# Two retention steps beside each group of scans, and the output projection's weights on the other side of SBUF

## The chip, the core and the metric

The kernel runs on one NeuronCore of one Trainium2 chip as a single launch. The metric is the device time of one execution in microseconds (us). Every execution has five engines with a queue each: TensorE (PE; its weight loads are listed as PEld), VectorE (DVE), ScalarE (ACT), GpSimd (POOL) and SyncE (SP), which issues most of the transfers between HBM and the on-chip memory SBUF.

## The reference

Two transformer blocks over 1024 tokens of width 1024. The part that matters here is the middle of the first block: a token mixer with two halves, whose results are joined, projected and routed to experts.

```python
def token_mix(h, hc, w_in, ..., w_out, need_ctx):
    u, uc = h @ w_in, hc @ w_in
    ret_lat, ret_ctx = retention_group(u[..., :RET_COLS], uc[..., :RET_COLS], need_ctx)
    rw = depthwise_conv(u[..., RET_COLS:], conv_w)
    rwc = depthwise_conv(uc[..., RET_COLS:], conv_w)
    rwkv_lat, rwkv_ctx = rwkv_group(rw, rwc, w0, w2, a0, a2, g2, k_k, k_a, r_k, lnx_w, lnx_b, need_ctx)
    lat = jnp.concatenate([ret_lat, rwkv_lat], axis=-1).astype(h.dtype) @ w_out
...
def first_block(...):
        x = x + gt1 * rms_norm(mix, g_post_mix)
        h2 = rms_norm(x, g_pre_ffn) * (1.0 + sc2) + sh2
        x = x + gt2 * rms_norm(ec_moe(h2, w_router[i], w_gate[i], w_up[i], w_down[i]), g_post_ffn)
```

`retention_group` is linear attention with a fixed decay per head in both directions over chunks of 128 tokens. `rwkv_group` is a recurrent scan, `S = S * w + (S a) b + v k`, in both directions; its result is normalised, gated (`g_f`, `g_b`) and added. `mix` is the product with `w_out`; `ec_moe` picks tokens by a router and runs 16 experts.

## The kernel before, in words

The kernel is written as Python generators whose code order is the program order; a scheduler then sets the order in each engine's queue, and each queue runs strictly in that order. Tiles come from pools. A pool lies on the left or on the right side of SBUF; a pool opened later on the same side takes the memory that an earlier one gave back, and its first write waits until the last reader of that memory is done.

The scan (`phase_chain`) is cut into 20 groups: 4 head pairs times one context group and 4 latent groups of 4 chunks of 64 tokens (names such as `UT_331` are group 3, pair 3, direction 1). A group has a preparation for each direction (scores `psc`, transposes `pb` and `pa`, the products `pm`, `px`, `pw`, `pg`, ending in `GQ`) and then four steps of the state: two products into `pc` (L826, L830) and the decay on VectorE, `S` (L835). ScalarE copies the outputs to `yst`, and SP stores them to `Yd` (L848, two transfers for each latent group; context groups store nothing). These pools lie on the left.

The retention (`phase_retention`) is a generator of 20 steps, 10 for each half of the heads: one rotates the keys (`kT`, L909), one builds the chunk states (`KV`, L917 to L930), and eight work on 128 tokens each (the score product `rs`, L957; the store to `LatD`, L986). On the token steps with odd index it also runs one of eight parts of `phase_mod2` (L204 to L216), which computes rows that scale the mix. Its pools lie on the right. The first 6 groups run beside the end of the input projection. The last 14 run beside the retention, by the loop in `first`: 1 step after an even group, 2 after an odd one, so 20 steps end with the last group.

`phase_out` follows. `gates(blk)` prepares 256 tokens: it loads `LatD`, the gate inputs `SGd`, `Yd` and `BV`, and makes the transposed left operand `lTh` and `lTl` (high and low halves) in two stages `q`, each with a square, a sum, a power on GpSimd, a product (`gyn`, L1057), a transpose (`yT`, L1063) and the gating (`z`). The output weights `w_out` come in 8 pieces (`woraw`); each is split into a high part by ScalarE (`wohi`) and a low part (`wolo`) by GpSimd for the first 4 and by VectorE for the other 4. The product is three matmuls for each piece into `mo`; ScalarE copies the result to `mix` (L1152), and norms, router, top-k and experts follow. Two tiles of 128 tokens make one block, and each tile has two halves of 512 columns. In this version the pools of the gates (`gnC`, `gnT`, `ouL`) lie on the right, where the retention was, and those of the weights, of the output tiles and of the rows (`ouW`, `ouT`, `ouG`) on the left, where the scan was.

Of the kernel before, what the change touches and what calls it, by code (L numbers as in the profile page):

```python
# [878 lines left out]
def phase_retention(E, A, tabs, others):  # L879
# [15 lines left out]
    for hh in range(2):  # L895
# [40 lines left out]
        for t in range(8):  # L936
            q = tp.tile([P, 1, 4, C], F32, tag="q", name=f"q{hh}_{t}s")
            nc.gpsimd.dma_start(q.rearrange("p o h d -> p (o h d)"), E.RD["q"][t * P:(t + 1) * P, cols])
            do_rope(q, t, 1, f"q{hh}_{t}")
            pk = bank(f"qTp{hh}_{t}")  # L940
            for j in range(2):
                nc.tensor.transpose(pk[:, j * P:(j + 1) * P], q[:, 0, 2 * j:2 * j + 2].rearrange("p h d -> p (h d)"), E.ident)
            qT, kv = qTs[t % 2], kvs[t % 2]
            qd = tp.tile([P, 2, 2, P], F32, tag="qd", name=f"qd{hh}_{t}")
            pkv = pk[:, :256].rearrange("p (j t) -> p j t", j=2)
            sp = (9 if t == 0 else t - 1, 8 if t == 7 else t + 1)
            for h in range(2):
                hs = slice(64 * h, 64 * h + 64)
                nc.scalar.copy(qT[hs, :, h], pkv[hs])
                for d in range(2):  # L950
                    nc.scalar.copy(kv[hs, :, d, h], KV[hs, :, sp[d], d])
            for d in range(2):
                nc.vector.tensor_mul(qd[:, d], pkv, qdec[:, 2 * hh:2 * hh + 2, d])
            psc = bank(f"rs{hh}_{t}")
            sv = psc.rearrange("p (j h t) -> p j h t", j=2, h=2)
            for j in range(2):
                nc.tensor.matmul(sv[:, j].rearrange("p h t -> p (h t)"), kT[:, t, j, :],  # L957
                                 qT[:, j].rearrange("p h t -> p (h t)"), start=True, stop=True)
            pm = tp.tile([P, 2, 2, 2, P], F32, tag="pm", bufs=1, name=f"pm{hh}_{t}")
            for j in range(2):  # L960
                for h in range(2):
                    nc.vector.tensor_mul(pm[:, j, h], sv[:, j, h].unsqueeze(1).to_broadcast([P, 2, P]),
                                         dmask[:, 4 * hh + 2 * j + h])
            yb = bank(f"y_{hh}_{t}")
            yv = yb.rearrange("p (h d v) -> p h d v", h=4, d=2)
            for j in range(2):
                for d in range(2):
                    nc.tensor.matmul(yv[:, 2 * j:2 * j + 2, d], qd[:, d, j], kv[:, j, d], start=True, stop=False)
                    for h in range(2):
                        nc.tensor.matmul(yv[:, 2 * j + h, d], pm[:, j, h, d], vt[:, t, 2 * j + h, :], start=False, stop=h == 1)  # L970
            nc.scalar.copy(Y[:, t], yv)
            sq = tp.tile([P, 8, C], F32, tag="ysq", bufs=1, name=f"ysq{hh}_{t}")
            yv = Y[:, t].rearrange("p h d v -> p (h d) v")
            nc.scalar.activation(sq, yv, AF.Square)
            ss = tp.tile([P, 8], F32, tag="yss", name=f"yss{hh}_{t}")
            nc.vector.tensor_reduce(ss, sq, axis=AX.X, op=OP.add)
            r = rstd_col(E, tp, ss, 8, 1.0 / C, 1e-6, f"yr{hh}_{t}")
            nc.vector.tensor_mul(yv, yv, r.unsqueeze(2).to_broadcast([P, 8, C]))
            g = tp.tile([P, 2, 4, C], F32, tag="gs", name=f"gs{hh}_{t}")
            for d in range(2):  # L980
                nc.gpsimd.dma_start(g[:, d].rearrange("p h v -> p (h v)"), E.RD["fb"[d]][t * P:(t + 1) * P, cols])
            nc.scalar.activation(g, g, AF.Silu)
            for d in range(2):
                nc.gpsimd.tensor_mul(g[:, d], g[:, d], Y[:, t, :, d, :])
            nc.vector.tensor_add(g[:, 0], g[:, 0], g[:, 1])
            nc.gpsimd.dma_start(E.LatD[t * P:(t + 1) * P, cols], g[:, 0].rearrange("p h d -> p (h d)"))  # L986
            if t % 2:
                others.pop(0)()
            yield


def phase_out(E, A):
# [3 lines left out]
    nc, tc = E.nc, E.tc  # L996
    with ExitStack() as st:
        pt = st.enter_context(tc.tile_pool(name="ouP", bufs=2, space=PSUM))
        cst = st.enter_context(tc.tile_pool(name="gnC", bufs=1, side="right"))
        tp = st.enter_context(tc.tile_pool(name="gnT", bufs=2, side="right"))  # L1000
        pg = st.enter_context(tc.tile_pool(name="gnP", bufs=2, space=PSUM))
        lp = st.enter_context(tc.tile_pool(name="ouL", bufs=2, side="right"))
        wp = st.enter_context(tc.tile_pool(name="ouW", bufs=1))
        py = st.enter_context(tc.tile_pool(name="gnY", bufs=1, space=PSUM))
        to = st.enter_context(tc.tile_pool(name="ouT", bufs=2))
        po = st.enter_context(tc.tile_pool(name="ouO", bufs=2, space=PSUM))
        rp = st.enter_context(tc.tile_pool(name="ouG", bufs=1))

        g2 = cst.tile([P, 2, 2, 2, 2, C], F32, name="g2")
        for d in range(2):  # L1010
# [74 lines left out]
                    split_hl(E, zv[:, 0], lTh[:, 4 + h + 2 * q], lTl[:, 4 + h + 2 * q])  # L1085
            return lTh, lTl

        lT = [gates(0)]
        wo = A.w_out[0]
        rw = wo[512:1024].rearrange("(p h v) f -> p h v f", p=NPAIR, h=2)  # L1090
        wts = []
        for k in range(KD):
            raw = wp.tile([P, D], F32, tag="raw", bufs=3, name=f"woraw{k}")
            hi = wp.tile([P, D], F32R, name=f"wohi{k}")
            lo = wp.tile([P, D], F32R, name=f"wolo{k}")
            if k < 4:
                nc.sync.dma_start(raw, wo[k * P:(k + 1) * P])
            else:
                h, q = k % 2, (k - 4) // 2 * 2
                for a in range(2):  # L1100
                    nc.sync.dma_start(raw[64 * a:64 * a + 64], rw[q + a, h])
            nc.scalar.copy(hi, raw)
            (nc.gpsimd if k < 4 else nc.vector).tensor_sub(lo, raw, hi)
            wts.append((hi, lo))
        g1 = bc_row(E, rp, 0, "g1row")
        s2r = bc_row(E, rp, 1, "s2row")
        sh2 = bc_row(E, rp, 2, "sh2row")
# [1362 lines left out]
def first(E, A):  # L2470
    nc, tc, ctx = E.nc, E.tc, E.ctx
    dt = lambda n: E.dram.tile([T, D], F32, name=n)
    E.x1d, E.h2d, E.accd = dt("x1d"), dt("h2d"), dt("accd")
    E.Td = [E.dram.tile([64, C, C], F32, name=f"Td{g}") for g in range(5)]
    E.gv = E.const.tile([P, 16], F32, name="gv")
    E.idx = E.const.tile([P, 16], I32, name="idx")
    with tc.tile_pool(name="rwk", bufs=1) as E.rwk:


        with ExitStack() as st:  # L2480
            ent = st.enter_context
            E.hpool = ent(tc.tile_pool(name="hp", bufs=1, side="right"))
            wide = ExitStack()
            in_project(E, A, (ent(tc.tile_pool(name="inW", bufs=1, side="right")), ent(tc.tile_pool(name="inE", bufs=3, side="right")),
                              wide.enter_context(tc.tile_pool(name="inP", bufs=4, space=PSUM, side="right"))))
            E.pss = ExitStack()
            E.ps_small = E.pss.enter_context(tc.tile_pool(name="pssm", bufs=1, space=PSUM))
            start(E, A)
            last = phase_in(E, A)
            wide.close()  # L2490
            E.in_pools = E.in_pools[:2] + (ent(tc.tile_pool(name="inP2", bufs=2, space=PSUM, side="right")),)
            cs = ExitStack()
            run = phase_chain(E, A, cs)
            for i, f in enumerate(last):
                if i % 4 == 0:
                    next(run)
                f()
        with ExitStack() as E.rst:
            E.rps = E.rst.enter_context(tc.tile_pool(name="reP", bufs=2, space=PSUM, side="right"))
            tabs = ret_setup(E)  # L2500
            ret = phase_retention(E, A, tabs, phase_mod2(E, A))
            for i, _ in enumerate(run):
                for _ in range(1 + i % 2):
                    next(ret, None)
            for _ in ret:
                pass
            cs.close()
    E.const = ctx.enter_context(tc.tile_pool(name="const2", bufs=1))
    E.mks = ctx.enter_context(ExitStack())
    E.mkp = E.mks.enter_context(tc.tile_pool(name="mkv", bufs=1))  # L2510
    with tc.tile_pool(name="ap", bufs=1) as ap_:
        E.affT = ap_.tile([64, T // 2], F32, name="affT")
        phase_out(E, A)
        with tc.tile_pool(name="tkT", bufs=1) as tk, tc.tile_pool(name="tkP", bufs=1, space=PSUM) as tkp:
            phase_topk(E, tk, tkp)
            setup2(E, A, tk)
    phase_moe1(E, A)
# [91 lines left out]
```

## Time and profile before

| | us |
|---|---|
| median of 3 runs (4094.79 to 4105.12) | 4097.06 |
| profiled execution, its own time | 4104.47 |
| its span, first to last instruction | 4102.7 |
| TensorE busy | 3776.7 (92%) |
| VectorE busy | 2718.3 (66%) |
| ScalarE busy | 2135.5 (52%) |
| GpSimd busy | 826.6 (20%) |

The table gives the average over stages that differ. The change touches the stretch from about 797 us (the first group beside the retention) to about 1426 us (the end of the output projection). A row of a stretch gives its length, then for TensorE, its weight loads, VectorE, ScalarE and GpSimd in this order the busy time and, in brackets, the count of instructions; then the granted TensorE clock as a share of full speed, the busy share of the transfer engines and GB/s. In a timeline a row begins with the start and the length; the end in square brackets is idle time of that engine before it, and what ended it.

### The profile page before, as it was taken

How to read it: one execution, taken by the hardware profiler on the slowest of the kernel's cores; microseconds unless marked ns; L12 is line 12 of the kernel's file. 1: busy time of each engine (PE TensorE's matmuls, PEld its weight loads, DVE VectorE, ACT ScalarE, POOL GpSimd, SP SyncE). 2: the span in 40 equal slices, each digit the busy share in tenths (PEclk: the TensorE clock that was granted, in tenths of full speed). 3: DMA queues.
4: the chain of work that ended last, by engine and by line, in shares of the span. 5: the costliest groups of instructions: out<-in, count | busy, mean ns of one | idle time of the engine just before them, and what ended most of it. 6: DMA issues, size and time to landing. Idle time of an engine off the chain costs nothing. (4 is left out here: it accounts for less than half of the span.)

```text
span 4102.7 us, 61718 instructions
## 1 busy us (share of the span) xinstructions
PE 3776.7 (92%) x23138; PEld 3126.6 (76%) x23138; DVE 2718.3 (66%) x4777; ACT 2135.5 (52%) x3389; POOL 826.6 (20%) x1054
## 2 busy tenths in 40 slices
PE   7989889898887889999969998999998999999998
PEld 5777788777766658777747788898886777788876
DVE  4576774377766578888865413667644356899987
ACT  4443312232324357777668513667643243788886
POOL 2333420244434120010010001222200022221110
PEclk9999999998998899999989999999999999999999
DMA  7556554455445489999741122111125326899998
GB/s 249 155 173 182 156 136 105 136 138 145 110 117 171 163 341 382 385 379 378 254 150 49 53 62 69 34 50 37 38 66 182 134 72 223 316 382 387 382 382 305
DMA packets 503960, 782.78 MB, mean 191 GB/s; under 512 B 199697, under 2 KB 334810, under 8 KB 502506
## 3 DMA queue, kind: packets, MB, share of 16 engines
q1 hardware_dynamic: 412298, 610.50, 42.5%
q0 software_dynamic: 40816, 138.37, 11.5%
q10 hardware_dynamic: 50544, 29.92, 2.4%
q8 instruction: 184, 3.01, 0.3%
q14 instruction: 118, 0.97, 0.1%
HBM read 646.28 MB, written 132.43 MB: 190 GB/s over the span
## 5 line engine op out<-in xcount | busy, mean ns | idle before, releaser
L2327 DVE TENSOR_TENSOR m2l<-m2r,m2h 128x1024 fp32r<-128x1024 f32 x380 | 449.6, 1223 | 52.5 <-ACT m2h L2326 48.5
L1260 DVE TENSOR_TENSOR m1l<-m1r,m1h 128x2048 fp32r<-128x2048 f32 x189 | 427.2, 2289 | 70.6 <-ACT m1h L1259 68.9
L2326 ACT CAST m2h<-m2r 128x1024 fp32r<-128x1024 f32 x384 | 394.7, 1051 | 84.2 <-PE m2g L109 35.6
L1259 ACT CAST m1h<-m1r 128x2048 fp32r<-128x2048 f32 x192 | 362.6, 1918 | 109.1 <-PE gu L109 81.4
L108 PE MATMUL m2g<-m2l,m2thx 128*128 128x512 f32 x512 | 202.5, 395 | 1.3 <-DVE m2l L2327 0.8
L107 PE MATMUL m2g<-m2h,m2thx 128*128 128x512 f32 x512 | 202.9, 405 | 0.3 <-ACT m2h L2326 0.3
L109 PE MATMUL m2g<-m2h,m2tlx 128*128 128x512 f32 x512 | 201.5, 393 | 0.0
L108 PE MATMUL gu<-m1l,xh 128*128 128x512 f32 x512 | 200.1, 396 | 0.2 <-DVE m1l L1260 0.2
L109 PE MATMUL gu<-m1h,xl 128*128 128x512 f32 x512 | 199.0, 394 | 0.0
L107 PE MATMUL gu<-m1h,xh 128*128 128x512 f32 x512 | 181.8, 397 | 10.1 <-ACT xh L60 6.0
L107 PE MATMUL apqk<-atW_hi,hT2h 128*128 128x256 f32 x512 | 145.2, 284 | 0.0
L108 PE MATMUL apqk<-atW_lo,hT2h 128*128 128x256 f32 x512 | 145.0, 283 | 0.0
L109 PE MATMUL apqk<-atW_hi,hT2l 128*128 128x256 f32 x512 | 144.8, 283 | 0.0
L107 PE MATMUL u_ps<-hTh,inW_hi 128*128 128x512 f32 (+1 forms) x336 | 128.3, 382 | 6.7 <-ACT inW_hi L91 6.7
L2379 POOL DMA_INDIRECT out_dram<-m2y,did x32 | 68.9, 2153 | 297.7 <-ACT m2y L2378 297.7
L108 PE MATMUL u_ps<-hTl,inW_hi 128*128 128x512 f32 (+1 forms) x336 | 125.9, 375 | 0.1
L109 PE MATMUL u_ps<-hTh,inW_lo 128*128 128x512 f32 (+1 forms) x336 | 124.9, 373 | 0.0
L107 PEld LDWEIGHTS gu<-m1h,xh 128*128 128x128 f32 x512 | 94.8, 188 | 34.3 <-ACT xh L60 8.1
L108 PEld LDWEIGHTS gu<-m1l,xh 128*128 128x128 f32 x512 | 96.4, 188 | 27.5 <-DVE m1l L1260 7.6
L108 PEld LDWEIGHTS m2g<-m2l,m2thx 128*128 128x128 f32 x512 | 96.8, 189 | 24.6 <-DVE m2l L2327 5.9
L1697 DVE TENSOR_SCALAR_CACHE_REDUCE pr<-sc 128x512 f32<-128x512 f32 (+2 forms) x192 | 103.7, 551 | 17.1 <-PE sc L1693 14.4
L1281 POOL DMA_INDIRECT accd<-y,idx x16 | 28.7, 1794 | 418.9 <-ACT y L1280 383.5
(1216 smaller groups left out, 11655.1 us busy)
## 6 DMA issues: line engine op xcount, KB each, us to landing
m2r<-in_w_gate_up_dram SPq DMA_DIRECT2D x128, 1024.0 KB
m1r<-in_w_gate_dram SPq DMA_DIRECT2D x64, 1024.0 KB
m1r<-in_w_up_dram SPq DMA_DIRECT2D x64, 1024.0 KB
m1r<-in_w_down_dram SPq DMA_DIRECT2D x64, 1024.0 KB
m2r<-in_w_down_dram SPq DMA_DIRECT2D x64, 1024.0 KB
inW_raw<-in_w_in_dram SPq DMA_DIRECT2D x72, 256.0 KB
m2w<-in_w_mod_dram POOLq DMA_DIRECT2D x32, 512.0 KB, 4.5
luW_raw<-in_w_in_dram SPq DMA_DIRECT2D x24, 512.0 KB
```

What stands on the lines that cost most here:

```text
L107: nc.tensor.matmul(ps, lh, rh, start=start, stop=False)
L108: nc.tensor.matmul(ps, lh, rl, start=False, stop=False)
L109: nc.tensor.matmul(ps, ll, rh, start=False, stop=stop)
L1259: nc.scalar.copy(hi, raw)
L1260: (nc.gpsimd if i < 3 else nc.vector).tensor_sub(lo, raw, hi)
L1281: nc.gpsimd.indirect_dma_start(out=E.accd, out_offset=bass.IndirectOffsetOnAxis(ap=E.idx[:, e:e + 1], axis=0), in_=y, in_offset=None, comp ...
L1697: nc.vector.tensor_scalar(pr[:, m, n0:n1], ps[m][:, :n], -1.0, None, op0=OP.mult, op1=OP.min, accum_out=s[:, 4 * i + m:4 * i + m + 1])
L2326: nc.scalar.copy(hi, raw[:, j])
L2327: (nc.gpsimd if i in (0, 2) else nc.vector).tensor_sub(lo, raw[:, j], hi)
L2379: nc.gpsimd.indirect_dma_start(out=E.x4d, out_offset=bass.IndirectOffsetOnAxis(ap=col, axis=0), in_=y, in_offset=None, compute_op=OP.add)
```

## The change

Three edits. After each of the last 14 groups the loop takes 2 steps of the retention, so its 20 steps stand beside 10 groups and the last 4 groups have none. The parts of `phase_mod2` run on even token steps instead of odd ones. In `phase_out` the two sets of pools change sides, and the code that loads and splits the weights stands ahead of `gates(0)`.

```diff
@@ phase_retention
-            if t % 2:
+            if t % 2 == 0:
                 others.pop(0)()
@@ phase_out
-        cst = st.enter_context(tc.tile_pool(name="gnC", bufs=1, side="right"))
-        tp = st.enter_context(tc.tile_pool(name="gnT", bufs=2, side="right"))
+        cst = st.enter_context(tc.tile_pool(name="gnC", bufs=1))
+        tp = st.enter_context(tc.tile_pool(name="gnT", bufs=2))
...
-        lp = st.enter_context(tc.tile_pool(name="ouL", bufs=2, side="right"))
-        wp = st.enter_context(tc.tile_pool(name="ouW", bufs=1))
+        lp = st.enter_context(tc.tile_pool(name="ouL", bufs=2))
+        wp = st.enter_context(tc.tile_pool(name="ouW", bufs=1, side="right"))
...
-        to = st.enter_context(tc.tile_pool(name="ouT", bufs=2))
+        to = st.enter_context(tc.tile_pool(name="ouT", bufs=2, side="right"))
...
-        rp = st.enter_context(tc.tile_pool(name="ouG", bufs=1))
+        rp = st.enter_context(tc.tile_pool(name="ouG", bufs=1, side="right"))
...
-        lT = [gates(0)]
         wo = A.w_out[0]
...
             wts.append((hi, lo))
+        lT = [gates(0)]
@@ first
-            for i, _ in enumerate(run):
-                for _ in range(1 + i % 2):
+            for _ in run:
+                for _ in range(2):
                     next(ret, None)
```

SP's queue at the end of the scan, before. `yst33` and `yst43` are the outputs of the last two groups; `g2`, `lt`, `gsg`, `gy` and `bv` are loads of the first block of gates.

```order
L848 DMA Yd_5525<-yst33_12562 128x256 x2
L1014 DMA g2_13041<-in_rwkv_g2_dram 128x2x64 x8
L1034 DMA lt0_13065<-LatD_8535 128x512
L1042 DMA gsg0_13083<-SGd0_792 128x256
L1047 DMA gy00_13086<-Yd_5525 128x2x256 x2
L848 DMA Yd_5525<-yst43_12853 128x256 x2
L1072 DMA bv000_13113<-BV0_783 64x256
L1047 DMA gy01_13142<-Yd_5525 128x2x256 x2
L1097 DMA woraw0_13198<-in_w_out_dram 128x1024
```

The same place now (the last weight piece is in two halves, of which one stands ahead of the gates' loads and one behind).

```order
L1096 DMA woraw0_13063<-in_w_out_dram 128x1024
L1096 DMA woraw2_13075<-in_w_out_dram 128x1024
L848 DMA Yd_5525<-yst33_12703 128x256 x2
L1096 DMA woraw3_13081<-in_w_out_dram 128x1024
L1100 DMA woraw6_13101<-in_w_out_dram 64x1024 x2
L1014 DMA g2_13041<-in_rwkv_g2_dram 128x2x64
L848 DMA Yd_5525<-yst43_12936 128x256 x2
L1014 DMA g2_13041<-in_rwkv_g2_dram 128x2x64 x7
L1100 DMA woraw7_13108<-in_w_out_dram 64x1024
L1034 DMA lt0_13117<-LatD_8535 128x512
L1042 DMA gsg0_13135<-SGd0_792 128x256
L1047 DMA gy00_13138<-Yd_5525 128x2x256 x2
```

The weights moved from behind the last store of the scan to ahead of it, and the gates' loads, all but one piece of `g2`, from ahead of it to behind it.

VectorE's queue over the four state steps of the last group, before. `S430` to `S433` are the steps; `Y1`, `gs1_7` are the last token step of the retention, `m2b31` the last part of `phase_mod2`.

```order
L835 TENSOR_TENSOR S430_12861<-pc430_12854,PT4_5552 128x128 x2
L978 TENSOR_TENSOR Y1_11256<-Y1_11256,yr1_7_rstd_12951 128x512
L211 TENSOR_TENSOR m2b31_12979<-m2b31_12979,m2ps31_12981 1x512
L835 TENSOR_TENSOR S431_12873<-pc431_12866,PT4_5552 128x128 x2
L985 TENSOR_TENSOR gs1_7_12954<-gs1_7_12954 128x256
L1025 COPY lncols_13061<-lnps_13059 128x8
L835 TENSOR_TENSOR S432_12885<-pc432_12878,PT4_5552 128x128 x2
L215 SCALAR_TENSOR_TENSOR m2b31_12979<-m2b31_12979,m2a31_12962 1x512
L835 TENSOR_TENSOR S433_12897<-pc433_12890,PT4_5552 128x128 x2
```

The same place now.

```order
L835 TENSOR_TENSOR S430_12944<-pc430_12937,PT4_5552 128x128 x2
L1102 TENSOR_TENSOR wolo4_13089<-woraw4_13087,wohi4_13088 128x1024
L835 TENSOR_TENSOR S431_12956<-pc431_12949,PT4_5552 128x128 x2
L835 TENSOR_TENSOR S432_12968<-pc432_12961,PT4_5552 128x128 x2
L1102 TENSOR_TENSOR wolo5_13096<-woraw5_13094,wohi5_13095 128x1024
L835 TENSOR_TENSOR S433_12980<-pc433_12973,PT4_5552 128x128 x2
```

Two splits of the weights stand between the steps where parts of the retention and of `phase_mod2` stood.

## Rows read from the trace of the kernel before

**Rows 1.** Stretches: length, PE, PEld, DVE, ACT, POOL, clock, transfers.
```profile
640.00:735.00 95.00, 94.93 (x1043) 82.88 (x1043) 43.26 (x128) 24.25 (x68) 3.67 (x6) 1.00 0.39 101
797.00:1222.00 425.00, 379.55 (x3811) 311.19 (x3811) 319.50 (x828) 138.77 (x366) 174.64 (x222) 0.92 0.50 129
1222.00:1281.00 59.00, 36.42 (x128) 25.85 (x126) 34.58 (x46) 20.40 (x31) 24.54 (x14) 0.74 0.63 184
1281.00:1426.00 145.00, 127.31 (x632) 105.90 (x633) 84.52 (x161) 59.26 (x117) 34.06 (x32) 0.88 0.44 151
```
**Rows 2.** SP's timeline, stores of latent groups: start, length, operation.
```profile
667.63 0.82 SPq L848 DMA_DIRECT2D Yd<-yst  x2
...
704.15 0.82 SPq L848 DMA_DIRECT2D Yd<-yst  x2
...
827.22 1.10 SPq L848 DMA_DIRECT2D Yd<-yst  x2
849.41 1.62 SPq L848 DMA_DIRECT2D Yd<-yst  x2
...
911.45 0.80 SPq L848 DMA_DIRECT2D Yd<-yst  x2
...
1004.09 1.25 SPq L848 DMA_DIRECT2D Yd<-yst  x2
1040.99 0.81 SPq L848 DMA_DIRECT2D Yd<-yst  x2
1075.48 0.80 SPq L848 DMA_DIRECT2D Yd<-yst  x2
...
1222.57 1.59 SPq L848 DMA_DIRECT2D Yd<-yst  x2
```
**Rows 3.** Busy time by engine in two pairs of groups (columns as in the first group).
```profile
847.00:909.00 62.00, 56.64 (x583) 47.68 (x581) 48.46 (x135) 24.23 (x68) 25.23 (x33) 0.97 0.46 118
1004.00:1075.00 71.00, 61.40 (x622) 49.96 (x622) 55.21 (x142) 22.83 (x61) 31.05 (x36) 0.90 0.52 134
```
**Rows 4.** TensorE's timeline, first and last retention step of each pair.
```profile
855.20 1.13 PE L957 MATMUL rs<-rqT,kT 128*128 128x256 f32 x4
...
899.47 1.13 PE L957 MATMUL rs<-rqT,kT 128*128 128x256 f32 x4
...
1018.49 1.11 PE L909 MATMUL kTp<-ident,kt 128*128 128x128 f32 x4 [0.31 <-DVE kt L893]
...
1071.12 1.13 PE L957 MATMUL rs<-rqT,kT 128*128 128x256 f32 x4
```
**Rows 5.** SP's timeline, loads of the first block of gates.
```profile
1207.78 4.67 SPq L1014 DMA_DIRECT2D g<-in_rwkv_g_dram  x8
...
1219.51 0.96 SPq L1047 DMA_DIRECT2D gy<-Yd  x2
```
**Rows 6.** What TensorE waited for, 1222 to 1300 us: total, times, longest.
```profile
PE yT L1063 <- DVE gyn L1057: 13.1, 4, 6.3
PE mo L108 <- POOL wolo L1103: 5.6, 2, 4.3
PE mo L107 <- ACT wohi L1102: 4.8, 3, 2.6
```
**Rows 7.** ScalarE's timeline, second halves of the first two output tiles.
```profile
1267.10 0.59 ACT L1152 COPY mix<-mo 128x512 f32<-128x512 f32 x1 [0.27 <-PE mo L109]
...
1290.22 0.59 ACT L1152 COPY mix<-mo 128x512 f32<-128x512 f32 x1 [3.94 <-PE mo L109]
```
**Rows 8.** Timelines of VectorE and GpSimd, first block of gates and weight splits.
```profile
1231.09 1.29 DVE L1057 TENSOR_TENSOR gyn<-gy,gr_rstd 128x512 f32<-128x512 f32 x2 [2.19 <-POOL gr_rstd L118]
...
1244.46 5.59 DVE L1057 TENSOR_TENSOR gyn<-gy,gr_rstd 128x512 f32<-128x512 f32 x2 [2.79 <-POOL gr_rstd L118]
...
1263.71 1.22 DVE L1103 TENSOR_TENSOR wolo<-woraw,wohi 128x1024 fp32r<-128x1024 f32 x1 [3.58 <-ACT wohi L1102]
...
1244.40 7.86 POOL L1103 TENSOR_TENSOR wolo<-woraw,wohi 128x1024 fp32r<-128x1024 f32 x3
```

## Prediction

> **What bounds the kernel now.** I read the busy times by stretch first, then the spacing of SP's stores, the timelines of TensorE and VectorE, and TensorE's waits. The change touches two stages. In the first, 797 to 1222 us, scans run beside the retention; TensorE is busy 379.55 of 425 us, VectorE 319.50, at a granted clock of 0.92 [rows 1]. So TensorE is nearly the bound, and a better order can win at most the tenth that it idles. Earlier, from 640 to 735, scans ran beside the input projection with TensorE busy 94.93 of 95 [rows 1]; the stores at 667.63 and 704.15 enclose two groups, 36.52 us or 18.26 a group [rows 2]. That is my price of a group without retention, though matmuls of the projection are in it, so a group by itself may be shorter.
>
> The second stage is the output projection. Its first 59 us are thin: TensorE busy 36.42 at a clock of 0.74, then 127.31 of 145 [rows 1]. There TensorE waits 13.1 us for `gyn`, which the transposes `yT` need, and for the split weights 5.6 (GpSimd) and 4.8 (ScalarE) [rows 6]. The change removes the last two and makes the loads behind the first later.
>
> **Two steps beside a group.** No step is added or taken away; the same 20 stand otherwise. From the store at 827.22 to the last at 1222.57 are 395.35 us and 13 groups with 19 steps [rows 2]; 13 groups at 18.26 are 237.38, so a step beside a group costs (395.35 - 237.38)/19 = 8.31. If that holds for every step, the change moves the scan's end by nothing: what the last four groups save, the first ten pay.
>
> The new pattern, two steps a group, stands by chance in the old order as well: between the stores at 849.41 and 911.45 are two groups and four token steps (the score product at 855.20 opens the first, that at 899.47 the last), at a clock of 0.97 [rows 2 to 4]. 62.04 us less 36.52 leave 25.52, or 6.38 a step. Between 1004.09 and 1075.48 are also four, the rotation and the chunk states among them, at 0.90 [rows 2 to 4]: 71.39 less 36.52 are 34.87, or 8.72. The first of those groups alone, with those two steps, took 36.90 (to 1040.99) [rows 2]: 18.64 over 18.26, or 9.32 a step.
>
> Four steps of the 20 are of the rotating kind and 16 token steps; one falls before 827.22, so 15 token steps remain. At 8.72 and 6.38 they make 4 x 8.72 + 15 x 6.38 = 130.6, against 157.97 now: the scan would end 27.4 us earlier. All 19 at 8.72 make 165.7, 7.7 later; at 9.32, 177.1, 19.1 later. At the stage's clock the 62.04 would be 62.04 x 0.97/0.92 = 65.4, so 7.22 a token step and 143.2 in all, 14.7 earlier. I take half way between this and nothing, **-7 us**: TensorE's busy share in the dense pair, 56.64 of 62 or 91% [rows 3], is hardly above the stage's 89%, and idle time given to the last four groups is lost again.
>
> What hides nothing any more is the cover of those four groups: TensorE's waits in a state step (two products, the decay on VectorE, the next products) have had retention matmuls in them, and now have none.
>
> **The splits inside the scan.** `wolo4` and `wolo5` stand between the last four `S`, at 1.22 us each [rows 8], 2.44 in all. They take the place of five small operations, which the order shows, so I count 0. But what `wolo` costs beside GpSimd is not constant: the `gyn` pair took 1.29 us alone and 5.59 while GpSimd ran three of its `wolo` (7.86 from 1244.40) [rows 8], 4.33 times as long. GpSimd's four splits now run beside the end of the scan. Were both VectorE splits stretched so, they would take 10.6, 8.1 more. The page "GPSIMD Engine Reference" of the Trainium skill, section "8. Key points", says that the two engines share their access to SBUF and that VectorE instructions with two SBUF inputs suffer; `gyn` has two, and its two durations agree; the decays `S` read PSUM for one input and would be spared. ScalarE's six casts stand between the copies of the scan's outputs; ScalarE is busy 138.77 of 425 [rows 1], so I let them hide; if each held up a copy, and the copy the next product, by a `wolo`'s 1.22, it would be 7.3. Both bounds together are 0 to 15; I take **+2**, near the low end because the time between the `S` is mostly waiting.
>
> **The output projection.** Let E be the last `Yd` store, now 1222.57. The second halves of the first two tiles are copied at 1267.10 and 1290.22 [rows 7], E + 44.5 and E + 67.7. The weights no longer wait: they are asked for before E, in memory that the retention has left. The gates' loads, however, now follow the store. Before, `gy00` was issued at 1219.51, E - 3.1 [rows 5]. Now ahead of it stand the store (1.59) [rows 2], seven eighths of the `g2` loads (4.67 x 7/8 = 4.1) [rows 5], and half a weight piece, `lt` and `gsg`, at about a store's 0.8 each (estimated): E + 8.1, so 11.2 later. The first `gyn` pair ended at 1231.09 + 1.29, E + 9.8, and the second at 1244.46 + 5.59, E + 27.5 [rows 8]. The first goes to E + 21.0. The second followed by 17.7, of which 4.3 were the stretch beside GpSimd's `wolo`, gone now: E + 34.4.
>
> From there to the first tile's copy were 17.0, with most of the 10.4 of weight waits in them. Taking three quarters of these out gives 9.2 and the first tile at E + 43.6, 0.9 earlier. For the second tile: TensorE's 36.42 us at 0.74 are 27.0 at full speed, about 13.5 for each of the two tiles, so E + 57.1, 10.6 earlier. After that TensorE is busy 88% and catches only what it lacked, and the gates of the next block, issued late as well, can hold it. If nothing of the weight waits comes out, the first tile is 6.9 late; if all, 1.7 early, and the second tile's 10.6 may carry through whole. Bounds -11 to +7; I take **-5**.
>
> **Other edits.** The eight parts of `phase_mod2` run a step earlier each with the same instructions, hidden by VectorE's idle quarter: 0; if that cover is lacking in the dense groups it is in the step price above. After 1426 the order is the same, and later stages shift whole.
>
> Sum: -7 + 2 - 5 = -10 from the profiled execution's 4104.47, so 4094.5. The median is 7.4 below that execution; the same below gives **4087**.
>
> **Rivals.** First, the dense pattern is cheap (0.18). Steps cost 6.38 and the rotating ones 8.72, the scan ends 27.4 earlier, and with the rest (-3) the time is 4097 - 30 = 4067. For it: the pair at 62.04. Against: its clock of 0.97 was better than the stage's, and 15 such steps in a row have not been seen. A group by itself under 18.26 would lead there too, since four of them are left alone.
>
> Second, nothing is gained (0.20). Price 8.31 holds, so the dense groups pay what the thin ones save, and `gyn`, 11.2 later, takes the place of the weights as the wait before the first tile. Then 0 to +7: 4097 to 4104, 4100 as its value. For it: TensorE's waits were longer on `gyn` (13.1) than on the weights (10.4) [rows 6]. The change does what it says, but its prize is then hidden.
>
> Third, slower by crowding (0.10). The state steps queue on VectorE behind the operations of two retention steps, and each costs 9.32 as in the group up to 1040.99. The scan ends 19.1 later, and with -3 the time is 4113. It decides from the step price at which 19 steps outweigh the rest by the measurable amount: 8.31 + 15.3/19 = 9.1. For it: VectorE is busy 48.46 and 55.21 in the pairs, 78% [rows 3], with chained waits. Against: three of four groups seen were cheaper.
>
> Fourth, slower by a thin end (0.10). The last four groups, without filler, run at a lower granted clock. The stretch after 1222, where TensorE worked in bursts between waits, had 0.74, between the two levels of 1.2 and 2.4 GHz [rows 1]. At 0.74 a group costs 18.26/0.74 = 24.7, four of them 25.7 more; with the forecast's -10 that is 4113. It decides from a clock of 0.76: there 4 x 18.26 x (1/0.76 - 1) = 23 outweighs the forecast's gain and the measurable difference. The page "TensorE: Matmul & The Clock Gate", section "HAM oscillation — how this bites in real kernels", of the Trainium skill says that bursts between waits start throttled again and again; the 0.74 agrees with it, and by that rule this rival would be the likeliest. Against: in a group the waits are short ones of one engine for another, and with the scan the clock was 1.00 from 640 to 735 [rows 1], though with filler.
>
> **How the numbers follow.** The forecast has 0.42; its own range is 4078 to 4097, by -17 to +2 in the sum's terms. What a measurement tells from no change is about 0.3%, 12.3 us: 4084.8 to 4109.4. Of the forecast 0.19 lies below that and 0.23 inside, the first rival is faster, the second is the same, and the two slower ones count fully as slower: faster 0.37, same 0.43, slower 0.20. The range 4062 to 4113 leaves out the far half of the first rival's cheap end and of the two slow ones.
>
> **What would show it.** The stores in the first ten groups: spacing near 33 us is the forecast's (18.26 + 2 x 7.2 to 7.8), 31 the first rival, 35 the second, 37 the third. The last four: 18 to 19 us each at a clock above 0.9; 24 the fourth rival. The last store should stand some 5 us earlier. TensorE's waits on `wolo` and `wohi` should be gone, those on `gyn` longer, and the first two copies at E + 44 and E + 57. The forecast is wrong if the last store moves by over 15 either way, if the second copy is no closer to E than now, or if a stage after 1426 changes its own length.

## The result and the profile after

The changed kernel takes 4129.96 us (median of 5 runs, 4126.55 to 4131.69) against 4097.06 before; the ratio is 1.0072, 95% interval [1.0054, 1.0090]. It is slower; the forecast of 4087 and its range, which ended at 4113, were wrong.

The profiled executions, 4131.61 against 4104.47, are 27.1 us apart. By stage: the last `Yd` store comes 41.7 us later; from it to the last copy of the output projection are 176.0 us where there were 181.6, so 36.1 are left there; between 3076 and 3480 us, where both kernels have the same code, the distance falls from 36 to 27. That execution of the kernel before was 7.4 above its median, so I give this last difference no cause.

SP's stores of the scan in the changed kernel (start, length), which answer to [rows 2]:

```profile
829.12 0.81 SPq L848 DMA_DIRECT2D Yd<-yst  x2
859.37 0.80 SPq L848 DMA_DIRECT2D Yd<-yst  x2
896.61 0.80 SPq L848 DMA_DIRECT2D Yd<-yst  x2
928.93 0.95 SPq L848 DMA_DIRECT2D Yd<-yst  x2
1014.66 1.00 SPq L848 DMA_DIRECT2D Yd<-yst  x2
...
1130.24 0.82 SPq L848 DMA_DIRECT2D Yd<-yst  x2
1208.76 0.80 SPq L848 DMA_DIRECT2D Yd<-yst  x2
1228.52 0.80 SPq L848 DMA_DIRECT2D Yd<-yst  x2
1247.15 0.80 SPq L848 DMA_DIRECT2D Yd<-yst  x2
1264.28 0.93 SPq L848 DMA_DIRECT2D Yd<-yst  x2
```

Up to 1130.24 are 8 groups with 16 steps: (301.12 - 8 x 18.26)/16 = 9.69 a step, above the 8.31 of before. The next 78.5 us hold two groups and the end of the retention; then three groups stand 17 to 20 apart. Stretches of the same kernel, the columns as in [rows 1]:

```profile
829.10:1264.30 435.20, 363.43 (x3512) 297.63 (x3512) 297.33 (x774) 133.25 (x346) 164.41 (x203) 0.87 0.46 121
...
859.40:1130.20 270.80, 222.09 (x2037) 183.69 (x2036) 189.62 (x482) 82.71 (x218) 121.48 (x157) 0.85 0.50 129
1130.20:1190.00 59.80, 47.40 (x425) 35.49 (x425) 39.56 (x101) 13.02 (x31) 19.38 (x28) 0.77 0.29 81
1190.00:1264.30 74.30, 67.40 (x785) 56.97 (x785) 41.73 (x121) 23.89 (x62) 9.99 (x5) 1.00 0.44 122
1264.30:1323.00 58.70, 39.29 (x163) 31.11 (x164) 29.81 (x57) 17.91 (x30) 18.67 (x13) 0.83 0.55 166
1323.00:1465.00 142.00, 123.83 (x614) 101.01 (x613) 81.89 (x154) 57.05 (x114) 28.25 (x29) 0.89 0.42 144
```

and the stage of the scans in the kernel before, between the same two stores:

```profile
827.20:1222.60 395.40, 354.10 (x3530) 290.05 (x3531) 295.74 (x773) 127.80 (x343) 157.67 (x201) 0.91 0.49 127
```

TensorE idles 71.8 us of the stage (435.2 - 363.4) where it idled 41.3. Busy time times granted clock, an estimate of its work at full speed, is 322 before and 316 after: about the same work, done with more waits and at a lower clock. The clock is 0.85 where two steps stand beside a group (859 to 1130 us) and 1.00 behind them.

TensorE's waits in this stage (for whom: total, times, longest), after and then before:

```profile
PE pc L826 <- DVE S L835: 13.7, 16, 3.1
PE m2ps L210 <- DVE m2a L204: 12.6, 3, 6.0
PE pm L761 <- DVE UT L738: 6.9, 1, 6.9
...
PE pm L761 <- DVE UV L793: 6.1, 5, 1.7
```

```profile
PE pc L826 <- DVE S L835: 9.3, 9, 2.3
PE m2ps L210 <- DVE m2a L204: 4.0, 2, 2.8
...
PE pm L761 <- DVE UV L793: 2.3, 2, 2.1
```

Summed over all such rows, TensorE waits 54.5 us for VectorE after and 26.2 before. The longest shows how. VectorE's timeline at the place:

```profile
1163.78 0.75 DVE L204 SCALAR_TENSOR_TENSOR m2a<-m2w,cs,m2a 128x512 f32<-128x512 f32 x1
...
1166.12 0.69 DVE L978 TENSOR_TENSOR Y<-Y,yr_rstd 128x512 f32<-128x512 f32 x1
1166.73 0.75 DVE L204 SCALAR_TENSOR_TENSOR m2a<-m2w,cs,m2a 128x512 f32<-128x512 f32 x1
1168.77 0.43 DVE L985 TENSOR_TENSOR gs<-gs 128x256 f32<-128x256 f32 x1 [1.29 <-POOL gs L984]
1169.11 0.75 DVE L204 SCALAR_TENSOR_TENSOR m2a<-m2w,cs,m2a 128x512 f32<-128x512 f32 x1
1169.77 0.42 DVE L893 TENSOR_TENSOR q_7s<-q_7s,rtq 128x256 f32<-128x256 f32 x1
1170.33 0.75 DVE L204 SCALAR_TENSOR_TENSOR m2a<-m2w,cs,m2a 128x512 f32<-128x512 f32 x1
1171.12 0.42 DVE L738 TENSOR_TENSOR UT<-psc,scmask 128x256 f32<-128x256 f32 x1
```

`UT` belongs to the scan. In VectorE's queue it stands behind three operations of the retention (`Y`, `gs`, `q_7s`), of which one waits for GpSimd, and four terms of a `phase_mod2` sum. TensorE's next product waits for it:

```profile
1171.69 0.34 PE L761 MATMUL pm<-UV,UT 64*64 64x64 f32 x1 [6.89 <-DVE UT L738]
```

and what the clock does there:

```profile
1158.00:1162.00 4.00, 3.53 (x36) 2.65 (x36) 3.12 (x9) 1.22 (x2) 0.31 (x1) 0.90 0.00 0
1162.00:1166.00 4.00, 2.34 (x20) 1.58 (x20) 3.10 (x11) 0.58 (x1) 2.04 (x1) 0.50 0.07 16
1166.00:1171.00 5.00, 0.00 (x0) 0.00 (x0) 3.54 (x7) 0.00 (x0) 3.14 (x5) 0.50 0.58 170
1171.00:1178.00 7.00, 6.31 (x20) 3.15 (x21) 2.93 (x7) 0.73 (x2) 0.53 (x1) 0.50 0.01 3
1178.00:1186.00 8.00, 7.53 (x80) 6.12 (x80) 5.00 (x14) 2.53 (x5) 1.22 (x2) 0.98 0.27 66
```

The clock is at its lower level (0.50) from 1162 on, when TensorE still worked 2.34 of 4 us. TensorE does nothing from 1166 to 1171, works the next 7 us at the lower level, and only then has the upper one back. So this idle stretch did not bring the lower level; what did is not shown.

In the output stage the waits for the split weights [rows 6] are gone, and two others stand in their place. TensorE's waits from 1264 us, and ScalarE's copies of the first two tiles (second halves, which answer to [rows 7]) and of the last:

```profile
PE yT L1063 <- DVE gyn L1057: 10.0, 5, 2.9
PE lnps L1023 <- DMA lnrows<-in_rwkv_lnx_b_dram: 7.7, 1, 7.7
PE ltp L1037 <- DMA lt<-LatD: 3.2, 2, 3.0
```

```profile
1307.25 0.59 ACT L1152 COPY mix<-mo 128x512 f32<-128x512 f32 x1 [0.82 <-PE mo L109]
...
1326.89 0.58 ACT L1152 COPY mix<-mo 128x512 f32<-128x512 f32 x1
...
1440.32 0.59 ACT L1152 COPY mix<-mo 128x512 f32<-128x512 f32 x1 [5.03 <-PE mo L109]
```

With E = 1264.28 the first tile is at E + 43.0, the second at E + 62.6. `lnrows`, the rows of the gates' norm, now load into memory of the scan; their transpose stands first in TensorE's queue behind it. That wait costs nothing by itself, because the next product waits a further 3.0 us for `lt`.

### The profile page after: what moved, and what is told of

It reads as the page before. It is cut to its first block, busy times and chain, and to the rows that moved or that the text cites. A ratio compares the mean times of both kernels' runs of the same rounds, so it can differ in the third digit from the quotient of the medians.

```text
span 4129.7 us, 61770 instructions
## 1 busy us (share of the span) xinstructions
PE 3785.6 (92%) x23138; PEld 3136.4 (76%) x23138; DVE 2709.7 (66%) x4777; ACT 2132.2 (52%) x3389; POOL 820.5 (20%) x1054
```

## The experiments

Last store, TensorE's idle time from the first store (near 828) to the last, and last store to last copy, each from one profile; the ratio is against runs of the kernel before on the same chip. A last store also carries some us that no edit made: the store ahead of the loop, at 734.99 in the kernel before, comes between 730.6 and 739.8 in these profiles, though the code up to there is the same.

| kernel | last store | idle | output | ratio, 95% interval |
|---|---|---|---|---|
| before | 1222.6 | 41.3 | 181.6 | |
| changed | 1264.3 | 71.8 | 176.0 | 1.0072 [1.0054, 1.0090] |
| e1 old pace | 1236.2 | 47.6 | 193.7 | 1.0051 [1.0033, 1.0069] |
| e2 pace only | 1283.6 | 57.8 | 164.0 | 1.0096 [1.0070, 1.0123] |
| e4 parts only | 1230.8 | 44.8 | 175.7 | 1.0028 [1.0013, 1.0043] |
| e8 no swap | 1266.6 | 69.6 | 164.3 | 1.0061 [1.0041, 1.0081] |
| e9 odd parts | 1258.0 | 56.2 | 174.9 | 1.0078 [1.0054, 1.0102] |
| e5 add on GpSimd | 1263.6 | 62.3 | 177.7 | 1.0045 [1.0031, 1.0059] |
| e6 parts beside thin | 1265.7 | 54.6 | 190.5 | 1.0113 [1.0088, 1.0138] |
| e10 twos first | 1243.1 | 43.9 | 175.7 | 1.0028 [1.0015, 1.0042] |
| e11 add, before | 1232.0 | 45.5 | 173.8 | 1.0000 [0.9986, 1.0013] |
| e12 two, one | 1250.5 | 53.5 | 168.5 | 1.0018 [1.0005, 1.0030] |
| e14 two, one, add | 1232.0 | 41.3 | 168.0 | 0.9991 [0.9979, 1.0002] |
| f1 changed, cut | 1235.3 | 40.3 | 176.7 | 1.0003 [0.9989, 1.0017] |
| f2 before, cut | 1210.5 | 31.9 | 182.4 | 0.9967 [0.9952, 0.9981] |

**The parts of the change.** e1 takes the loop back in the changed kernel, e2 makes the loop's change alone, e4 that of the parts alone.

```diff
e1, on the changed kernel
-            for _ in run:
-                for _ in range(2):
+            for i, _ in enumerate(run):
+                for _ in range(1 + i % 2):
e2, on the kernel before
-            for i, _ in enumerate(run):
-                for _ in range(1 + i % 2):
+            for _ in run:
+                for _ in range(2):
e4, on the kernel before
-            if t % 2:
+            if t % 2 == 0:
```

> The changed kernel with the old loop: 1 step of the retention after an even group, 2 after an odd one; the pools stay on their new sides and the phase_mod2 parts on even steps. Theory A (the loss is the two-step pace: the retention has a pace of its own of about 20 us a token step, so ten groups are stretched to 38 us and four groups are left over behind it): the last Yd store is back within 8 us of 1222.57, the ratio to the kernel before is 0.996 to 1.002 (the output stage keeps the 5.6 us that it gained). Theory B (the pools' new sides, the early weights or the moved parts hold the scan up): the last store stays near 1264 and the ratio near 1.007.

> The kernel before with the new loop alone: 2 steps after each of the 14 groups; pools and parts as before. Theory A: last Yd store near 1264 (1255 to 1272), ratio 1.007 to 1.011, the groups with two steps 36 to 39 us apart, the last four 17 to 20. Theory B: last store near 1222, ratio 0.998 to 1.002.

> The kernel before with the phase_mod2 parts on even token steps alone. Theory A: ratio 0.998 to 1.002. If the parts matter (TensorE's wait for m2a was 12.6 us in the changed kernel against 4.0), last Yd store 5 to 10 us later and ratio 1.001 to 1.003.

The loop is what moves the scan's end: 61.1 us alone (e2), and taking it back gives 28.1 of 41.7 (e1). In the whole table the scans with the old loop end by 1236.2, and those with the new loop and all their work at 1258.0 or later. But e1 and e4 end 13.6 and 8.2 us later than before, and e1's ratio, 1.0051, is well off what theory A expected: the parts cost something at the old pace, as expected for the case that they matter, and the sides, with the weights' code that stands earlier, cost 18.0 in the output stage (193.7 against 175.7 in e4).

e2's ratio is in theory A's range, its last store is 11.6 us behind it. Its stage:

```profile
828.80:1283.60 454.80, 396.97 (x3547) 326.43 (x3548) 299.96 (x782) 131.72 (x347) 158.32 (x201) 0.82 0.45 122
```

Against the kernel before TensorE is idle 16.5 us more and busy 42.9 us more, at a clock of 0.82 against 0.91. It waits 36.6 us for VectorE, less than in the changed kernel (54.5). So in e2 most of the loss is about the same work at a lower clock, and waits for VectorE are not the whole account of what the loop costs.

e8 is the changed kernel with the pools on their old sides and the weights' code behind `gates(0)` again, e9 with `if t % 2:` again.

> The changed kernel with the pools back on their old sides (kernel before with the new loop and the parts on even steps). If the new sides cost in the output stage (the gates' loads now wait for the scan): the last mix copy comes 160 to 168 us after the last Yd store, as in e2_pace_only (164.0), where the changed kernel has 176.0; ratio 1.003 to 1.005. If the new sides help there, 176 or more and a ratio of 1.007 or more. The last store itself within 8 us of 1264.3 if the sides do not touch the scan.

> The changed kernel with the phase_mod2 parts on odd token steps as before. If the parity is what separates the changed kernel's scan from that of e2_pace_only (last store 1264.3 against 1283.6): last store 1275 to 1290, ratio 1.010 to 1.014. If it is the pools' sides: last store 1260 to 1268, ratio near 1.007.

With the parts on even steps the sides and the earlier weights' code, which e8 takes back together, cost 11.7 us in the output stage (176.0 against 164.3) and hardly move the scan's end (2.3). e8's store and its 164.3 are as expected for sides that cost; its ratio is above that range, and its interval overlaps the changed kernel's. The 5.6 that the stage gained are then 17.3 that come with the loop and the parts, less 11.7. That the retention's early end brings the 17.3 and the scan's memory takes the 11.7 is argued; e4, whose retention ends as before, already has a stage 5.9 shorter.

With the parts on odd steps it looks otherwise: e9 and e2 differ in the sides and the weights' code alone, and their scans end 25.6 us apart. e9's store is 2 us below the range given for the sides, its ratio near it, but with even parts the sides did nothing to the scan. So the effects don't add. The parity's effect is of the size by which one interleaving differs from the next, and its sign stays open.

**A step alone.** e3, on the kernel before, calls all groups first and the retention's code behind them.

```diff
-            for i, _ in enumerate(run):
-                for _ in range(1 + i % 2):
-                    next(ret, None)
+            for _ in run:
+                pass
```

> The kernel before with the retention's code behind all groups; the scheduler pulls about half of its steps up beside the scan, the second half of the heads runs alone behind it. This measures a step without a group beside it. Theory A (a chain of its own, one step behind the other): token steps alone are 16 to 20 us apart, store to store of LatD, with TensorE busy under 60%; the time is 80 to 130 us over the kernel before. Rival (crowding: a step costs 9 to 10 us only because it queues with a group's work, and no more alone): 7 to 10 us apart, time 10 to 40 us over.

The ratio is 1.0115 [1.0082, 1.0149], some 47 us over, between the two expectations. GpSimd's timeline of the token steps that run behind the scan, first and last of eight, and the stretch:

```profile
1200.24 0.61 POOL L986 DMA_DIRECT2D LatD<-gs  x1 [0.76 <-DVE gs L985]
...
1283.59 0.60 POOL L986 DMA_DIRECT2D LatD<-gs  x1 [0.76 <-DVE gs L985]
```

```profile
1192.00:1284.00 92.00, 62.16 (x224) 47.76 (x222) 57.31 (x121) 24.94 (x58) 54.05 (x70) 0.54 0.31 94
```

83.35/7 = 11.9 us a step: neither the 16 to 20 of theory A nor the rival's 7 to 10. With nothing beside it no engine is full (TensorE 68%), at a clock of 0.54; what sets the 11.9 was not tried. Theory A, a retention with a pace of 20 us, falls. As an estimate from these prices, in the old pace a group hid 11.9 - 8.3 = 3.6 of each step, in the new one 11.9 - 9.7 = 2.2.

**Which of VectorE's operations.** e5 moves one sum to GpSimd, e6 takes the parts from the token steps and puts two beside each of the last four groups. f1 and f2 leave 6 of the 8 terms of each part's sum out, in the changed kernel and in the kernel before.

```diff
e5
-            nc.vector.tensor_add(g[:, 0], g[:, 0], g[:, 1])
+            nc.gpsimd.tensor_add(g[:, 0], g[:, 0], g[:, 1])
e6
-            if t % 2 == 0:
-                others.pop(0)()
...
                     next(ret, None)
+                    if i > 9:
+                        parts.pop(0)()
f1, f2
-                if k + j:
+                if k + j == 7:
...
-                else:
+                elif k + j == 0:
```

> The changed kernel with one edit: the sum of the two directions of a token step (gs, L985) on GpSimd, which made its inputs, where VectorE did it after waiting for GpSimd. Theory C (VectorE's queue: operations of the retention that wait for GpSimd or a transfer stand ahead of the scan's, and TensorE waits for those): VectorE's wait for gs (10.3 us from 829 to 1190 in the changed kernel) is gone, the last Yd store comes 5 to 15 us before 1264.3, ratio to the kernel before 1.003 to 1.006. Rival (the steps' plain work or the retention's own chain sets the pace): the last store stays within 4 us of 1264.3, ratio 1.006 to 1.009.

> The changed kernel with the eight phase_mod2 parts taken from the token steps and put beside the last four groups, two parts to a group. Theory C: without the eight m2a sums and their waits for m2w in VectorE's queue the ten dense groups are 33 to 36 us apart where they were 38, the stretch from the fourth group of pair 2 to the first of pair 3 (78.6 us) shrinks by over 10; the thin groups grow from 18.5 to 20 to 23; last Yd store 1235 to 1252. Rival (the retention's own chain sets the pace): dense groups stay at 37 to 39 and the thin ones only get longer, last store 1264 to 1280.

> The changed kernel with 6 of the 8 products of each phase_mod2 part left out (the m2a sums have 2 terms; every load stays): 6 x 0.75 = 4.5 us of VectorE less in each of 8 parts, so the rows that scale the mix are not the reference's. If VectorE's queue is what a two-step group is long by: the ten dense groups shrink from 38 to 33 or 34 each and the last store comes 28 to 40 us before 1264.3 (1224 to 1236), TensorE's waits for VectorE fall from 54.5 us towards 25. If VectorE's time there is covered and TensorE's low clock or the retention's own chain sets the length: last store 1254 to 1268.

> The same cut in the kernel before. If the sums are better covered beside one step and two in turn than beside two: the last store comes only 5 to 15 us before 1222.6, a half or less of what the cut gives in the changed kernel. If VectorE's time is paid in full wherever it stands: 28 to 36 us earlier, as much as there.

e5's last store hardly moved (1263.6), as the rival expected, but its first store came 5.6 later (834.71), so its stage is 6.3 us shorter. Its ratio is in theory C's range, and its interval overlaps the changed kernel's; its profiled execution took 4136.5 against a median of 4119.4. TensorE's waits for VectorE fall from 54.5 to 33.5 us, and yet the stage gains at most some 6: the wait for `gs` is at most a small part of the later scan, and a wait that goes is not time won. In e6 the dense groups fell to 29 to 35 us, as expected or lower, but the last three grew to 24.5, 40.4 and 30.2: what the parts cost they cost there too, the stage ended no earlier (expected: 1235 to 1252), and the output stage grew by 14.5.

The cut shows how much of it is VectorE's work. The two stages:

```profile
828.50:1235.30 406.80, 366.52 (x3512) 302.95 (x3512) 263.76 (x726) 134.17 (x348) 160.10 (x202) 0.89 0.49 128
```

```profile
825.60:1210.50 384.90, 352.97 (x3525) 290.82 (x3521) 261.16 (x722) 127.93 (x342) 150.89 (x198) 0.92 0.50 126
```

48 terms of 0.75 us, 36 us of VectorE, are left out (its busy time falls by 33.6 and 34.6). They bring the last store 29.0 us forward in the changed kernel and 12.1 in the kernel before, both inside what the first theory expected, and the ratios agree (0.69% and 0.33%). TensorE's waits for VectorE fall from 54.5 to 27.6 and from 26.2 to 16.1. Beside one and two steps in turn two thirds of this work were hidden; beside two steps one fifth. That makes 16.9 of the 41.7. 24.8 stay between f1 and f2, and no run takes them apart: in f1's stage TensorE is idle some 8 us longer than in f2's and busy some 14 longer, at a clock of 0.89 against 0.92.

**The mixture and its order.** All on the kernel before: e10 takes `2 if i < 6 else 1` steps, e12 `2 - i % 2`, e11 has e5's edit, e14 those of e12 and e11.

> The kernel before with another order of the same mixture: 2 steps after each of the first 6 groups, then 1 after each of the last 8 (before: alternating, which makes 6 groups with two and 8 with one as well). Theory D (the price of a group is set by how many steps stand beside it and grows faster than linearly: about 18.5 us with none, 26 with one, 37 with two; so leaving groups empty loses and the order does not matter): last Yd store 1215 to 1232, ratio 0.997 to 1.003. Rival (full groups in a row are what loses, by steps that pile up and a clock that stays low; alternating ones recover): the first five spacings 38 to 43, last store 1236 or later, ratio 1.004 to 1.008.

> The kernel before with the loop's two counts exchanged: 2 steps after an even group, 1 after an odd one, so the 20 steps end with the thirteenth group and only the last has none. Theory D: 7 groups with two, 6 with one, 1 with none, 3 to 8 us more scan (last store 1222 to 1232); the output stage, whose gates find their memory free a group earlier, takes 166 to 176 us from the last store to the last mix copy where before took 181.6; ratio 0.996 to 1.001. Rival (the retention's early end gives the output stage nothing): 180 to 184 and ratio 1.001 to 1.004.

> The kernel before with the sum gs (L985) on GpSimd alone. If VectorE's waits for GpSimd hold up the scan in the old pace too: VectorE's wait for gs (9.8 us) is gone, last Yd store 3 to 10 us earlier, ratio 0.996 to 0.999. If they cost only where two steps stand beside a group: ratio 0.999 to 1.002.

> Both edits together, the exchanged counts and the sum gs on GpSimd, on the kernel before. If both give what is hoped of each: ratio 0.993 to 0.998. If neither does: 1.000 to 1.004.

e10 has the same mixture as before and ends 20.5 us later (15.7, counted from the store ahead of the loop), with spacings up to 47.5 where two steps stand beside a group. The store is in the rival's range, the ratio still inside theory D's, but clear of no change: the order counts, which theory D denied, by less than the rival said. e12, whose only difference is which of two groups comes first, ends 27.9 later, outside theory D's range, and gets half of it back in the output stage (168.5), where the retention is over a group earlier. The old loop was a favourable one among near neighbours. e11 ends 9.4 later, gets most of it back in the output stage, and its ratio is 1.0000: in the old pace the wait for `gs` costs nothing that can be measured. e14, at 0.9991 [0.9979, 1.0002], can't be told from the kernel before; no version here that does all the work beats it.

## Why the prediction was wrong

**The step that failed** is the price of the dense pattern, "25.52, or 6.38 a step" for the pair from 849.41 to 911.45, and with it the -7 for the scan's end. The count of four token steps holds for TensorE. What the pair lacked are the parts of `phase_mod2`, put at 0 because a lack of cover would be "in the step price above". A row of one line gives the length, the busy time and count on its engine (for TensorE the weight loads behind it), the clock and the transfers. TensorE's score products (L957) in the pair and in the stage before, then VectorE's terms of the sums (L204) in both:

```profile
849.41:911.45 62.04, 4.58 (x16) 2.71 (x16) 0.97 0.46 119
827.22:1222.57 395.35, 19.41 (x64) 11.29 (x64) 0.91 0.49 127
```

```profile
849.41:911.45 62.04, 3.93 (x6) 0.97 0.46 119
827.22:1222.57 395.35, 43.21 (x55) 0.91 0.49 127
```

16 of 64 products are four of the sixteen token steps. 6 of 55 terms are less than one of the eight parts, where four token steps in the new order bring two. So the price that was carried over to the whole scan held less than half of the parts that belong to it. What the runs show in its place: 9.69 a step up to 1130 us in the changed kernel, and (280.3 - 8 x 18.26)/16 = 8.39 over the same groups of f1, where most of the parts' sums are left out. By this the sums make some 1.3 of the 3.3 between 6.38 and 9.69. Why the rest of the pair's cheapness did not carry over to 16 steps in a row stays open; the clock was 0.97 in the pair and 0.85 from 859 to 1130 us. The sum has a slip beside this: the step ahead of 827.22 is the rotation, and the stores to `LatD` of all sixteen token steps come behind it (the first at 869.32), so 3 and 16 steps make 128.2 and not 130.6.

**The third rival** named a part of the mechanism: scan operations queue on VectorE behind two steps' operations. Its price of 9.32 measured 9.69 to 1130 us; what it lacked is the end, where the last three token steps and a context group took 59.8 us with TensorE at a clock of 0.77. So it gave 19.1 for the 41.7. I held against it that three of four groups were cheaper; two of these are the pair that lacked its parts. VectorE's idle quarter was read as cover for the parts; in a queue that runs in order, idle time elsewhere does not help the operation behind.

**The fourth rival** was wrong in place and sign: the last groups ran at 17 to 20 us and a clock of 1.00. The lower clock came in the dense groups. The rule cited there (the Trainium skill, "TensorE: Matmul & The Clock Gate", "HAM oscillation — how this bites in real kernels") tells of bursts between waits for transfers that each start throttled. The burst behind the wait for `UT` does start at 0.50, but the clock was there before that wait, so the trace agrees in part; I had applied the rule to the wrong groups. How much of the loss is the clock's own was not tried; e2 suggests that it can be the larger share.

**The output projection**, forecast -5, measured -5.6, held in its steps up to the first tile: `gy00` was issued at E + 7.9 (forecast 8.1), the two `gyn` pairs ended at E + 22.2 (21.0) and E + 32.8 (34.4), the first tile came at E + 43.0 (43.6).

```profile
1285.21 1.29 DVE L1057 TENSOR_TENSOR gyn<-gy,gr_rstd 128x512 f32<-128x512 f32 x2 [3.04 <-POOL gr_rstd L118]
...
1295.74 1.29 DVE L1057 TENSOR_TENSOR gyn<-gy,gr_rstd 128x512 f32<-128x512 f32 x2 [2.79 <-POOL gr_rstd L118]
```

The second tile came at E + 62.6 (57.1): between the two TensorE waited 4.3 us for `gyn` of the next block, which the prediction had named as what can hold it. TensorE's waits for `gyn` did not grow, though: 10.0 where [rows 6] have 13.1. That -5 and -5.6 lie so close is partly luck, because -5 was chosen between bounds of -11 and +7.

**The splits inside the scan** took nothing that shows: the last group, 17.1 us, is the shortest of the three. I took +2. **The parts** were costed at 0; at the old pace e4 measured 8.2 in the scan and 0.28% in all, and in the changed kernel most of their sums were worth 29.0 (f1).

## What to carry to other kernels

When a short stretch stands in for a pattern, count every kind of work in it, side jobs too: here the pair had its four token steps but less than half of its parts of `phase_mod2`. Where two chains share in-order queues, a bunch can hide less than the same work spread thinly: here a step cost 9.7 us where two stood beside each group and 8.3 in the old mixture, and groups left bare gave back less than the full ones lost. The order within a mixture counts as well (e10, e12), so try near neighbours before a rule is made of one. An early load is worth what it frees only if the memory that it takes was not the one in which another load was early.

## What the hardware showed unexpectedly

The same cut of 36 us of VectorE work was worth 12.1 us or 29.0 by what stood beside it, with VectorE busy 75% and 68% of the two stages. And busy time times granted clock, the estimate of TensorE's work at full speed, is 316 to 332 us in all fifteen kernels of the table, whose stages take 385 to 455 us (e2: 397 us busy at a clock of 0.82).
